# Regrouping tokens at the producers of layer 0's output projection, with norm passes in halves and the next row loaded a step ahead

## The chip, the cores and the metric

The kernel runs on one core of a Trainium2 chip. The metric is the device time of one execution in microseconds (us); lower is better. Engines are named as in the profile: PE is TensorE's matmuls and PEld its weight loads, DVE is VectorE, ACT is ScalarE, POOL is GpSimd, SP is SyncE, which issues all DMAs here.

## The reference, cut to what matters

One inference step of a two-layer recurrent trunk over a prompt of 2048 tokens, model width 1024, and eight single sample tokens, all in float32.

```python
def trunk(x, c, ...):
    for i in range(DEPTH):                       # DEPTH = 2
        shift, scale, gate = split(silu(c) @ mod_w[i] + mod_b[i])
        h = rms_norm(x, norm_w[i]) * (1.0 + scale) + shift
        y = ab_mixer(h, ...) if i % 2 == 0 else s5_mixer(h, ...)
        x = x + gate * y
    return rms_norm(x, final_norm_w), states
```

Layer 0 (`ab_mixer`) projects h to 6160 columns, runs eight RG-LRU heads and eight gated DeltaNet heads along the tokens, gates both with SiLU, and multiplies the 2048 columns of their outputs, y, with an output matrix. Layer 1 (`s5_mixer`) projects h to u and z, runs a diagonal state space model along the tokens, a GLU and an output projection. A final norm follows.

## The kernel before, in words

Activations lie with channels on the 128 partitions and tokens along the free axis, so that a model row of 1024 channels is eight tiles ("rows" k = 0 to 7) of 128 x 1024 tokens. The prompt is worked in two halves of 1024 tokens (`hf`), with the eight sample tokens riding along as columns 1024 to 1031 of one half. The order is: layer 0 for both halves, then layer 1 for both halves.

A float32 matrix product is made of three products of split operands (high and low part of weights and of data). `in_unit` (L863) is one output unit: it multiplies eight rows with eight weight blocks, three products each, for the column blocks in `blocks` (two of 512 columns, or 384, 384 and 264 where the sample columns ride along), accumulates in PSUM (tag "mm", four accumulators) and calls `evac` for each block, which evicts the accumulator. While it issues matmuls it pumps background generators, which trace the recurrences' work in between.

Layer 1's state space model wants the tokens of a half regrouped: instead of their natural order (n t), n = 0 to 127, t = 0 to 7, it wants (t n). Before the change, layer 0 works in natural order, and the regrouping happens in `make_h` (L426) for layer 1: it reads the row x at a step of eight elements (`perm`, L423) and writes h in regrouped order.

`make_h` prepares a stage's input. For each row k it gets x from `xsrc(k)` (which issues a load of 512 KB into a tile "xk"), scales it in place on VectorE (L430), writes the high part hh on ScalarE (L435) and the low part hl on VectorE (L436). It is a generator that yields after each row. `prep0` (L785) calls it for layer 0's second half, `prep1` (L1258) for both halves of layer 1.

Layer 0's outputs go through DRAM. The DeltaNet head's tail (L1158 to L1168) transposes the output back, multiplies it with its gate and stores it to `yd` in two pieces of 512 tokens; `lru` ends (L1205, L1206) with a product of 1024 tokens on POOL and a store to `yd`. `load_y` reads `yd` back and splits it into high and low parts.

`out_phase` (L1222) is the output projection of layer 0, with a first pass over the RG-LRU heads (`grp` 0) and a second over the DeltaNet heads (`grp` 1). Each pass has eight units m. In the first pass `acc[m]` is loaded from the input x; the eviction (L1231) adds gate times the product to it. In the second pass acc[m] is then stored to `x1d`, squared and summed, and after each unit one step (two after the first units) of the next stage's `make_h` is taken. The order of a stage is thus: unit m, store of x1 row m, sum of squares, then step k of `make_h`, whose x load is issued there and used at once. Layer 1's output phase (from L1892) has the same form: x1 row m+1 loaded for the residual, unit m, eviction (L1903, which reads x1 at the step of eight and writes x2 regrouped), sum of squares, store, then a step of `make_h` for the second half.

The program is traced into a tile framework that fixes at build time, from its own estimate of times and a priority that follows the order of tracing, in which order each engine gets its instructions, and gives out the slots of the pools: 35 slots of 1032 x 4 bytes ("a", `TA`), 20 of half the size ("b", `TB`). On the chip every engine's queue, SP's among them, is then worked in that order. `Ahead` (L117) wraps an engine so that its instructions get priority over 2000 others (`VH` is VectorE so wrapped).

Of the kernel before, what the change touches and what calls it, by code (L numbers as in the profile page):

```python
# [70 lines left out]
def hybrid_step(ctx: ExitStack, tc: tile.TileContext, I, O, dump=None):  # L71
# [42 lines left out]
    def dma(out, in_):  # L114
        SP.dma_start(out, in_)  # L115
# [30 lines left out]
    def f(x):  # L146
        return x.bitcast(FT)
# [33 lines left out]
    def wait(n):  # L181
        for _ in range(n):
            yield
# [236 lines left out]
        rsqrt(r, e, (128, 8), "rs8")  # L420
        return r

    def perm(ap):  # L423
        return ap.rearrange("p (n t) -> p t n", t=8)

    def make_h(i, xsrc, rows, hh, hl, permute, w):  # L426

        for k in range(8):
            x = xsrc(k)
            V.scalar_tensor_tensor(x, x, wsc[i][:, k, 0:1], rows, op0=OP.mult, op1=OP.mult)  # L430
            hh[k], hl[k] = TA("hh", FR, (128, w)), TA("hl", FR, (128, w))
            h_, l_ = hh[k][:, 0:HT], hl[k][:, 0:HT]
            if permute:
                x, h_, l_ = perm(x), *(t.rearrange("p (t n) -> p t n", t=8) for t in (h_, l_))
            A.activation(h_, x, AF.Identity, bias=mod[i][:, k, 0:1])  # L435
            V.scalar_tensor_tensor(l_, x, mod[i][:, k, 0:1], f(h_), op0=OP.add, op1=OP.subtract)  # L436
            yield

    def sample_norm(xs, name):
# [345 lines left out]
    def prep0(hf, hh, hl):  # L785
        rows = rows_from_cols(rstd_cols(ss0[hf], "rstd0"), 8)
        yield
        yield from make_h(0, xload(hf), rows, hh, hl, False, HT)

    def load_ba():  # L790
        wba = TB("wba", FT, (128, 8, 32))
# [243 lines left out]
    def gdn_main(hf, h, g):  # L1035
# [120 lines left out]
        rsqrt(ro, m, S8, "rs8")  # L1156
        V.tensor_tensor(o, o, bc(ro[:, :, None], C3), op=OP.mult)
        yield from wait(10)  # L1158
        for b in range(NB):
            ps = PS("pre", Q3)  # L1160
            for c in range(4):
                PE.transpose(ps[:, c, :], o[:, b * 4 + c, :], ident)
            sl = slice(b * 512, (b + 1) * 512)
            y = TB("yb")
            V.scalar_tensor_tensor(y, ps.rearrange("p a b -> p (a b)"), gnw[:, 0:1], zb[:, sl],
                                   op0=OP.mult, op1=OP.mult)
            dma(yd[hf, 8 + h][:, sl], y)
            yield from wait(2)  # L1168


    def lru_split(xc, n):
# [4 lines left out]
    def lru(hf, h, xc, sz, blocks, parts, dc):  # L1176
        (ghi, glo), = W.next()
        n = W1 if hf == 0 else HT
        xh, xl = parts.pop()
        gx, ga, tt = (TA(t_, FT, (128, n)) for t_ in ("gx", "ga", "tt"))  # L1180
        for b0, b1 in blocks:
            pg = [PS("mm", (128, b1 - b0)) for _ in range(2)]
            for j in range(2):
                c = slice(j * 128, j * 128 + 128)
                mm3(pg[j], ghi[:, c], glo[:, c], xh[:, b0:b1], xl[:, b0:b1], True, True)
            A.activation(ga[:, b0:b1], pg[1], AF.Sigmoid, bias=gab[:, h:h + 1])
            A.activation(gx[:, b0:b1], pg[0], AF.Sigmoid, bias=gxb[:, h:h + 1])
        A.activation(tt, ga, AF.Tanh, scale=sp4[:, h:h + 1])
        A.activation(ga, ga, AF.Exp, scale=spm8[:, h:h + 1])
        if dc is not None:  # L1190
            A.activation(dc, dc, AF.Exp)
        A.activation(tt, tt, AF.Sqrt)
        G.tensor_tensor(gx, gx, xc, op=OP.mult)
        V.scalar_tensor_tensor(tt, ga, 1.0, tt, op0=OP.add, op1=OP.mult)
        if hf == 0:
            V.memset(tt[:, 0:1], 1.0)
        G.tensor_tensor(gx, gx, tt, op=OP.mult)
        V.tensor_tensor_scan(tt[:, 0:HT], ga[:, 0:HT], gx[:, 0:HT], lru_h[:, h:h + 1],
                             op0=OP.mult, op1=OP.add)
        V.tensor_copy(lru_h[:, h:h + 1], tt[:, HT - 1:HT])  # L1200
        if hf == 0:
            V.tensor_tensor(slru[:, h, :], slru[:, h, :], ga[:, HT:W1], op=OP.mult)
            V.tensor_tensor(slru[:, h, :], slru[:, h, :], gx[:, HT:W1], op=OP.add)
            V.tensor_tensor(ys[:, h, :], slru[:, h, :], sz[:, HT:W1], op=OP.mult)
        G.tensor_tensor(sz[:, 0:HT], sz[:, 0:HT], tt[:, 0:HT], op=OP.mult)  # L1205
        dma(yd[hf, h], sz[:, 0:HT])  # L1206


    def load_y(hf, grp, yh, yl):
# [12 lines left out]
    def out_phase(hf, grp, blocks, yh, yl, acc, ahead):  # L1222
        sq = Squares()
        for m in range(8):
            if grp == 0:
                acc[m] = TA("acc")
                dma(acc[m], I["xt"][m][:, hf * HT:(hf + 1) * HT])

            def evac(b0, b1, p):
                e = min(b1, HT)  # L1230
                V.scalar_tensor_tensor(acc[m][:, b0:e], p[:, 0:e - b0], mod[0][:, 16 + m, 0:1],  # L1231
                                       acc[m][:, b0:e], op0=OP.mult, op1=OP.add)
                if b1 > HT:
                    t = TT("so", (128, 8))
                    V.tensor_tensor(t, p[:, e - b0:b1 - b0], mod[0][:, 16 + m, 1:9], op=OP.mult)
                    V.tensor_tensor(x1s[:, m, :], x1s[:, m, :], t, op=OP.add)

            in_unit(yh, yl, blocks, evac)
            if grp == 1:
                x1 = acc.pop(m)  # L1240
                dma(x1d[hf, m], x1)
                sq.add(x1)
            if m >= ahead[1]:
                for _ in range(2 if m < ahead[2] else 1):
                    next(ahead[0], None)
        if grp == 1:
            bg.add(finish_later(sq, ss1[hf]), "fin")
        for _ in ahead[0]:
            pass
# [8 lines left out]
    def prep1(hf, hh, hl):  # L1258
        rows = rows_from_cols(rstd_cols(ss1[hf], "rstd1"), 8)
        yield  # L1260
        yield from make_h(1, x1load(hf), rows, hh, hl, True, W1 if hf == 0 else HT)


    def sample0():
# [569 lines left out]
    for hf in range(2):  # L1834
# [64 lines left out]
        def evac_o(m):  # L1899
            def evac(b0, b1, p):  # L1900
                e = min(b1, HT)
                t0, t1 = b0 // 128, e // 128
                V.scalar_tensor_tensor(x2[m][:, b0:e].rearrange("p (t n) -> p t n", n=128),  # L1903
                                       p[:, 0:e - b0].rearrange("p (t n) -> p t n", n=128),
                                       mod[1][:, 16 + m, 0:1], perm(x1[m])[:, t0:t1, :],
                                       op0=OP.mult, op1=OP.add)
                if b1 > HT:
                    V.tensor_copy(Os[:, m, :], p[:, e - b0:b1 - b0])
            return evac
# [59 lines left out]
def layouts(x_prompt, x_sample, c_prompt, c_sample, state_conv_a, state_lru, state_conv_b,  # L1969
# [6 lines left out]
    def cols(v, n):  # L1976
# [5 lines left out]
        "xt": x.T.reshape(8, 128, SEQ),  # L1982
        "xst": x_sample[:, 0].T.reshape(8, 128, 8).transpose(1, 0, 2),
        "ct": np.concatenate([c_prompt, c_sample]).T.reshape(8, 128, 9).transpose(1, 0, 2),
        "modw": mod_w.reshape(2, 4, 2, 128, 6, 512).transpose(0, 4, 1, 3, 2, 5).reshape(2, 6, 4, 128, 1024),
        "modb": mod_b.reshape(2, 24, 128).transpose(2, 0, 1),
        "normw": norm_w.reshape(2, 8, 128).transpose(2, 0, 1),
# [82 lines left out]
```

## Time and profile before

| | us |
|---|---|
| median of 3 runs | 3206.87 |
| the three runs | 3198.5, 3206.87, 3208.52 |
| the profiled execution | 3189.97 |
| span of the profile, first to last instruction | 3188.1 |

The profile is of one execution. TensorE is busy 2953.1 us of the span, VectorE 2089.1, ScalarE 1122.4, POOL 696.7. The mean clock granted to TensorE is 0.966 of full speed. The stages that matter here, in us from the span's start: heads of layer 0, first half, about 75 to 930; its output projection 939 to 1158; heads of the second half to about 2000; its output projection 2011 to 2225; layer 1, first half, to 2727, with its output phase from 2623; layer 1, second half, to the end. Each engine is busy for the time stated, and idle times are given with what ended them; a unit's length is read from the start of its first matmul to the start of the next unit's.

### The profile page before, as it was taken

What the parts mean: (1) busy time and instruction counts of PE and PEld (TensorE: products, weight loads), DVE (VectorE), ACT (ScalarE), POOL (GpSimd) and SP (SyncE); (2) the same over time, 40 slices, a digit from 0 to 9 for tenths busy, and PEclk for the clock granted to TensorE, in tenths of its full rate; (3) what the DMA queues carried; (4) which work ended last, traced back from release to release, by engine and by line L of the source; (5) the groups of instructions that cost most, each with busy time, mean ns of one, the idle gap of its engine ahead of it and who ended that gap; (6) DMA issues with size and microseconds to landing.
All of it is one profiled execution on the core that took longest, in us unless ns stands there. A gap on an engine that the chain in (4) does not pass through costs nothing.

```text
span 3188.1 us, 53992 instructions
## 1 busy us (share of the span) xinstructions
PE 2953.1 (93%) x19958; PEld 2581.2 (81%) x19958; DVE 2089.1 (66%) x5420; ACT 1122.4 (35%) x1999; POOL 696.7 (22%) x672
## 2 busy tenths in 40 slices
PE   5999999999999999999999999998978899988998
PEld 3888888898888777777777778898878899777786
DVE  7896887677885767965766687345555534665525
ACT  3544445444443324433434444223111233201222
POOL 3233433224332322111111121101112222001100
PEclk8999999999989999999999999999989999999999
DMA  6344445344447853444444333565576547597442
GB/s 229 121 133 154 135 140 161 129 135 155 162 134 261 278 188 124 137 132 143 128 131 133 121 115 102 192 207 170 185 218 217 186 151 262 181 311 240 151 138 86
DMA packets 406440, 532.09 MB, mean 167 GB/s; under 512 B 143776, under 2 KB 210848, under 8 KB 406176
## 3 DMA queue, kind: packets, MB, share of 16 engines
q1 hardware_dynamic: 406176, 528.63, 50.8%
q8 instruction: 158, 2.59, 0.3%
q14 instruction: 106, 0.87, 0.1%
HBM read 328.11 MB, written 200.36 MB: 166 GB/s over the span
## 4 chain that ended last, share of the span: by engine, by line
PE 55%; DVE 27%; DMA 7%; issue 4%; ACT 3%; POOL 2%; SPq 2%; DVEq 0%; POOLq 0%; ACTq 0%
PE ps_mm L874 41%; DVE s5t L127 4%; DVE c_v L854 2%; DMA xk<-x1d 2%; SPq L115 2%; DVE xc L854 1%; DVE fsP L1002 1%; DVE c_q L854 1%; PE ps_pre L1783 1%; DVE fsT L1004 1%; ACT hh L435 1%; POOL wlo L234 1%; PE ps_pre L1725 1%; PE ps_ch L1137 1%; PE ps_pre L1782 1%
## 5 line engine op out<-in xcount | busy, mean ns | idle before, releaser
L874 PE MATMUL ps_mm<-hh,wlo 128*128 128x512 f32 (+2 forms) x2536 | 792.1, 373 | 0.0
L874 PE MATMUL ps_mm<-hh,whi 128*128 128x512 f32 (+2 forms) x2536 | 761.7, 361 | 4.4 <-DVE sz L1868 2.0
L874 PE MATMUL ps_mm<-hl,whi 128*128 128x512 f32 (+2 forms) x2536 | 748.7, 355 | 0.8 <-DVE hl L436 0.8
L874 PEld LDWEIGHTS ps_mm<-hl,whi 128*128 128x128 f32 x2536 | 479.6, 192 | 45.3 <-DVE hl L436 1.2
L874 PEld LDWEIGHTS ps_mm<-hh,whi 128*128 128x128 f32 x2536 | 472.6, 192 | 54.0 <-DVE sz L1868 2.5
L874 PEld LDWEIGHTS ps_mm<-hh,wlo 128*128 128x128 f32 x2536 | 449.9, 192 | 35.7 <-issue 7.4
L234 POOL TENSOR_TENSOR wlo<-wraw,whi 128x512 fp32r<-128x512 f32 (+1 forms) x200 | 280.9, 1411 | 639.1 <-ACT whi L233 408.4
L874 PE MATMUL ps_mm<-yh,whi 128*128 128x512 f32 (+2 forms) x640 | 187.2, 360 | 16.0 <-DVE acc L1231 8.0
L874 PE MATMUL ps_mm<-yl,whi 128*128 128x512 f32 (+2 forms) x640 | 189.1, 357 | 2.9 <-DVE yl L234 2.9
L874 PE MATMUL ps_mm<-yh,wlo 128*128 128x512 f32 (+2 forms) x640 | 190.8, 361 | 0.0
L233 ACT ACTIVATE whi<-wraw 128x512 fp32r<-128x512 f32 (+1 forms) x200 | 121.7, 617 | 104.4 <-DMA wraw<-in_w 47.6
L1134 ACT ACTIVATE qs<-ps_ch,geg 128x128 f32<-128x128 f32 x128 | 47.1, 368 | 287.6 <-DVE rr L1131 284.2
L874 PEld LDWEIGHTS ps_mm<-yh,whi 128*128 128x128 f32 x640 | 119.7, 192 | 29.5 <-ACT yh L233 9.3
L854 DVE SCALAR_TENSOR_TENSOR c_k<-raw,cbw,c_k 128x256 f32<-128x256 f32 x192 | 92.0, 517 | 63.3 <-ACT c_k L891 62.4
L874 PEld LDWEIGHTS ps_mm<-yl,whi 128*128 128x128 f32 x640 | 120.9, 192 | 15.3 <-DVE yl L234 3.9
L874 PEld LDWEIGHTS ps_mm<-yh,wlo 128*128 128x128 f32 x640 | 119.0, 192 | 9.7
L874 PE MATMUL ps_mm<-y2h,whi 128*128 128x384 f32 (+3 forms) x344 | 102.6, 345 | 7.4 <-DVE x L1903 7.4
L890 ACT ACTIVATE raw<-ps_mm 128x384 f32<-128x384 f32 (+1 forms) x160 | 81.6, 513 | 72.7 <-PE ps_mm L874 69.2
L874 PE MATMUL ps_mm<-y2h,wlo 128*128 128x384 f32 (+3 forms) x344 | 101.8, 345 | 0.0
L874 PE MATMUL ps_mm<-y2l,whi 128*128 128x384 f32 (+3 forms) x344 | 101.4, 344 | 0.0
L854 DVE SCALAR_TENSOR_TENSOR xc<-raw,caw,xc 128x256 f32<-128x256 f32 x192 | 95.6, 519 | 4.2 <-ACT xc L891 3.6
L854 DVE SCALAR_TENSOR_TENSOR c_v<-raw,cbw,c_v 128x256 f32<-128x256 f32 x192 | 95.4, 531 | 4.0 <-ACT c_v L891 3.8
(669 smaller groups left out, 5772.3 us busy)
## 6 DMA issues: line engine op xcount, KB each, us to landing
wraw<-in_w SPq DMA_DIRECT2D x128, 256.0 KB, 3.7
whw<-whi SPq DMA_DIRECT2D x128, 256.0 KB, 2.6
wlw<-wlo SPq DMA_DIRECT2D x128, 256.0 KB, 2.3
whi<-whw SPq DMA_DIRECT2D x128, 256.0 KB, 4.5
wlo<-wlw SPq DMA_DIRECT2D x128, 256.0 KB, 4.5
modw<-in_modw SPq DMA_DIRECT2D x48, 512.0 KB, 5.6
yk<-yd SPq DMA_DIRECT2D x32, 512.0 KB, 6.0
xk<-x1d SPq DMA_DIRECT2D x32, 512.0 KB, 5.4
```

What stands on the lines that cost most here:

```text
L115: SP.dma_start(out, in_)
L127: return getattr(self.eng, op)(*args, **kw)
L233: a = A.activation(hi, src, AF.Identity)
L234: return a, (lo_eng or V).tensor_tensor(lo, src, f(hi), op=OP.subtract)
L435: A.activation(h_, x, AF.Identity, bias=mod[i][:, k, 0:1])
L854: V.scalar_tensor_tensor(d, raw[:, a * n + j:a * n + j + n], wt[:, tile_i, j:j + 1], d, op0=OP.mult, op1=OP.add)
L874: PE.matmul(p, w[:, c], x[:, b0:b1], start=(k == 0 and x is hh[k] and w is wh), stop=(k == 7 and w is wl))
L890: A.activation(raw[:, 3 + b0:3 + e], p[:, 0:e - b0], AF.Copy)
L1002: V.tensor_tensor(pr_[:, 0:i, 0:i], Ti[:, 0:i, 0:i].rearrange("p j c -> p c j"), bc(F[:, 0:i, i].unsqueeze(1), s), op=OP.mult)
L1004: V.tensor_reduce(Ti[:, i, 0:i], pr_[:, 0:i, 0:i], axis=AX.X, op=OP.add, negate=True)
L1134: A.activation(qs, p1[:, 1, :], AF.Copy, scale=g["eg"][:, c:c + 1])
L1137: PE.matmul(p2_, U[:, c, :], rr, start=True, stop=True)
```

## The change

`make_h` no longer permutes. It issues the load of row k+1 before it works on row k, and works each row in two halves of 512 tokens. The tokens are regrouped earlier: the DeltaNet tail and the RG-LRU end write their outputs in (t n) order, that is with a step of 128 elements (512 bytes) between neighbours in time, and `acc` is loaded from `xp`, a copy of x that the host lays out in (t n) order. The DeltaNet tail collects both halves in one tile of the big pool and stores it with one DMA of 512 KB. The RG-LRU product goes to `gx` instead of `sz`. Both evictions (L1231, L1903) are issued through `VH`, and the one of layer 1 loses its permuted operand.

```diff
-    def perm(ap):
-        return ap.rearrange("p (n t) -> p t n", t=8)
-
-    def make_h(i, xsrc, rows, hh, hl, permute, w):
-
+    def by_t(ap):
+        return ap.rearrange("p (n t) -> p n t", t=8)
+
+    def make_h(i, xsrc, rows, hh, hl, w):
+
+        nxt = xsrc(0)
         for k in range(8):
-            x = xsrc(k)
-            V.scalar_tensor_tensor(x, x, wsc[i][:, k, 0:1], rows, op0=OP.mult, op1=OP.mult)
+            x = nxt
+            if k < 7:
+                nxt = xsrc(k + 1)
             hh[k], hl[k] = TA("hh", FR, (128, w)), TA("hl", FR, (128, w))
-            h_, l_ = hh[k][:, 0:HT], hl[k][:, 0:HT]
-            if permute:
-                x, h_, l_ = perm(x), *(t.rearrange("p (t n) -> p t n", t=8) for t in (h_, l_))
-            A.activation(h_, x, AF.Identity, bias=mod[i][:, k, 0:1])
-            V.scalar_tensor_tensor(l_, x, mod[i][:, k, 0:1], f(h_), op0=OP.add, op1=OP.subtract)
+            for c in (slice(0, HT // 2), slice(HT // 2, HT)):
+                x_, h_, l_ = x[:, c], hh[k][:, c], hl[k][:, c]
+                V.scalar_tensor_tensor(x_, x_, wsc[i][:, k, 0:1], rows[:, c], op0=OP.mult, op1=OP.mult)
+                A.activation(h_, x_, AF.Identity, bias=mod[i][:, k, 0:1])
+                V.scalar_tensor_tensor(l_, x_, mod[i][:, k, 0:1], f(h_), op0=OP.add, op1=OP.subtract)
             yield
...
+        y = TA("yb")
         for b in range(NB):
...
-            y = TB("yb")
-            V.scalar_tensor_tensor(y, ps.rearrange("p a b -> p (a b)"), gnw[:, 0:1], zb[:, sl],
+            V.scalar_tensor_tensor(y.rearrange("p (t n) -> p n t", t=8)[:, b * 64:(b + 1) * 64],
+                                   by_t(ps.rearrange("p a b -> p (a b)")), gnw[:, 0:1], by_t(zb[:, sl]),
                                    op0=OP.mult, op1=OP.mult)
-            dma(yd[hf, 8 + h][:, sl], y)
             yield from wait(2)
+        dma(yd[hf, 8 + h], y)
...
-        G.tensor_tensor(sz[:, 0:HT], sz[:, 0:HT], tt[:, 0:HT], op=OP.mult)
-        dma(yd[hf, h], sz[:, 0:HT])
+        G.tensor_tensor(gx[:, 0:HT].rearrange("p (t n) -> p n t", t=8), by_t(sz[:, 0:HT]), by_t(tt[:, 0:HT]),
+                        op=OP.mult)
+        dma(yd[hf, h], gx[:, 0:HT])
...
-                dma(acc[m], I["xt"][m][:, hf * HT:(hf + 1) * HT])
+                dma(acc[m], I["xp"][m][:, hf * HT:(hf + 1) * HT])
...
-                V.scalar_tensor_tensor(acc[m][:, b0:e], p[:, 0:e - b0], mod[0][:, 16 + m, 0:1],
+                VH.scalar_tensor_tensor(acc[m][:, b0:e], p[:, 0:e - b0], mod[0][:, 16 + m, 0:1],
...
-                t0, t1 = b0 // 128, e // 128
-                V.scalar_tensor_tensor(x2[m][:, b0:e].rearrange("p (t n) -> p t n", n=128),
-                                       p[:, 0:e - b0].rearrange("p (t n) -> p t n", n=128),
-                                       mod[1][:, 16 + m, 0:1], perm(x1[m])[:, t0:t1, :],
-                                       op0=OP.mult, op1=OP.add)
+                VH.scalar_tensor_tensor(x2[m][:, b0:e], p[:, 0:e - b0], mod[1][:, 16 + m, 0:1],
+                                        x1[m][:, b0:e], op0=OP.mult, op1=OP.add)
...
+        "xp": x.T.reshape(8, 128, 2, 128, 8).transpose(0, 1, 2, 4, 3).reshape(8, 128, 2048),
```

## Rows read from the trace of the kernel before

**Rows 1.** The page's first part: busy us (share of the span) and instructions of each engine.
```profile
PE 2953.1 (93%) x19958; PEld 2581.2 (81%) x19958; DVE 2089.1 (66%) x5420; ACT 1122.4 (35%) x1999; POOL 696.7 (22%) x672
```

**Rows 2.** The page's chain that ended last: share of the span by engine.
```profile
PE 55%; DVE 27%; DMA 7%; issue 4%; ACT 3%; POOL 2%; SPq 2%; DVEq 0%; POOLq 0%; ACTq 0%
```

**Rows 3.** Windows of units, layer 0's last output pass: length, busy (instructions) by engine, PEclk, DMA.
```profile
2145.40:2156.75 11.35, 11.35 (x74) 11.35 (x73) 6.47 (x8) 2.69 (x3) 0.00 (x0) 1.00 0.71 233
...
2168.10:2180.92 12.82, 11.59 (x75) 11.32 (x73) 7.60 (x10) 4.02 (x4) 1.28 (x1) 1.00 0.49 159
...
2192.59:2205.20 12.61, 11.59 (x75) 11.32 (x73) 6.23 (x9) 4.36 (x4) 4.08 (x2) 1.00 0.49 166
2205.20:2225.19 19.99, 14.20 (x75) 13.93 (x74) 9.73 (x13) 6.59 (x5) 3.85 (x2) 0.83 0.55 170
```

**Rows 4.** Windows of units, output phase of layer 1's first half.
```profile
2634.14:2645.48 11.34, 11.34 (x74) 11.34 (x73) 2.68 (x4) 3.71 (x6) 3.85 (x3) 1.00 0.95 311
...
2656.82:2671.96 15.14, 13.17 (x74) 12.90 (x73) 8.15 (x8) 5.15 (x5) 5.59 (x3) 0.89 0.82 282
2671.96:2684.55 12.59, 11.60 (x74) 11.34 (x73) 5.50 (x8) 4.05 (x3) 2.66 (x2) 1.00 0.72 252
2684.55:2700.19 15.64, 13.16 (x75) 12.90 (x73) 9.75 (x9) 3.38 (x2) 0.00 (x0) 0.89 0.52 171
...
2711.79:2727.02 15.23, 13.32 (x75) 12.98 (x73) 9.30 (x9) 3.38 (x2) 0.00 (x0) 0.89 0.43 139
```

**Rows 5.** Waits of PE, 2130 to 2226, then 2625 to 2745: total us, times, longest.
```profile
PE ps_mm L874 <- DVE acc L1231: 8.0, 3, 5.8
...
PE ps_mm L874 <- DVE x L1903: 7.4, 4, 2.5
```

**Rows 6.** Timeline of DVE in the longest unit: start, length, instruction, idle before it.
```profile
2205.15 1.28 DVE L430 SCALAR_TENSOR_TENSOR xk<-xk,wsc,rows 128x1024 f32<-128x1024 f32 x1 [2.92 <-DMA xk<-x1d]
2208.69 2.05 DVE L436 SCALAR_TENSOR_TENSOR hl<-xk,mod,hh 128x1024 fp32r<-128x1024 f32 x1 [2.26 <-ACT hh L435]
2210.67 1.52 DVE L1231 SCALAR_TENSOR_TENSOR acc<-ps_mm,mod,acc 128x384 f32<-128x384 f32 x3
```

**Rows 7.** Timeline of SP's queue before it.
```profile
2199.55 0.38 SPq L115 DMA_DIRECT2D x1d<-acc  x1
2199.99 0.43 SPq L115 DMA_DIRECT2D xk<-x1d  x1
```

**Rows 8.** Groups by form, 1080 to 1175, ACT: busy us, mean ns of one | idle before.
```profile
L435 ACT ACTIVATE hh<-xk,mod 128x1024 fp32r<-128x1024 f32 x8 | 9.2, 1152 | 36.8 <-DVE xk L430 28.5 <-DMA whi<-whw 8.2
```

**Rows 9.** Groups by form, 2630 to 2746.
```profile
L435 ACT ACTIVATE hh<-xk,mod 128x1024 fp32r<-128x1024 f32 x8 | 18.6, 2327 | 40.7 <-DVE xk L430 40.7
...
L436 DVE SCALAR_TENSOR_TENSOR hl<-xk,mod,hh 128x1024 fp32r<-128x1024 f32 x8 | 17.7, 2218 | 19.0 <-ACT hh L435 19.0
...
L1903 DVE SCALAR_TENSOR_TENSOR x<-ps_mm,mod,xk 128x384 f32<-128x384 f32 x16 | 14.6, 958 | 13.8 <-PE ps_mm L874 7.4 <-DMA wraw<-in_wo 6.4
```

**Rows 10.** Groups by form, whole span, DVE.
```profile
L1165 DVE SCALAR_TENSOR_TENSOR yb<-ps_pre,gnw,zbl 128x512 f32<-128x512 f32 x32 | 23.9, 746 | 13.9 <-PE ps_pre L1162 13.7
...
L1231 DVE SCALAR_TENSOR_TENSOR acc<-ps_mm,mod,acc 128x384 f32<-128x384 f32 x32 | 18.5, 611 | 14.9 <-PE ps_mm L874 9.1 <-DMA wlo<-wlwo 5.5
```

**Rows 11.** Timeline of DVE at the end of the program.
```profile
3173.52 1.42 DVE L1953 TENSOR_TENSOR x<-x,rows 128x256 f32<-128x256 f32 x4
3174.87 0.66 DVE L1903 SCALAR_TENSOR_TENSOR x<-ps_mm,mod,xk 128x256 f32<-128x256 f32 x1
```

**Rows 12.** The instructions of line 1205: shortest, median, longest ns; first and last start.
```profile
L1205 POOL TENSOR_TENSOR sz<-sz,tt x16: 2334/2373/2877, 165.2 to 2002.4; 128x1024 f32<-128x1024 f32 x16
```

**Rows 13.** Timelines of SP's queue and of PE where the second half's heads end.
```profile
2004.76 0.32 SPq L115 DMA_DIRECT2D yd<-sz  x1
...
2011.54 1.23 PE L874 MATMUL ps_mm<-yh,whi 128*128 128x384 f32 x3 [3.97 <-ACT yh L233]
```

**Rows 14.** The instructions on the tile yk: shortest, median, longest ns.
```profile
L234 DVE TENSOR_TENSOR yl<-yk,yh x32: 1217/1232/2315, 942.0 to 2129.0; 128x1024 fp32r<-128x1024 f32 x16, 128x1032 fp32r<-128x1032 f32 x16
```

More of the change, by code (lines that the diff above doesn't have):

```diff
@@ L787, in prep0 @@
         yield
-        yield from make_h(0, xload(hf), rows, hh, hl, False, HT)
+        yield from make_h(0, xload(hf), rows, hh, hl, HT)
     def load_ba():
@@ L1260, in prep1 @@
         yield
-        yield from make_h(1, x1load(hf), rows, hh, hl, True, W1 if hf == 0 else HT)
+        yield from make_h(1, x1load(hf), rows, hh, hl, W1 if hf == 0 else HT)
     def sample0():
```

## The prediction, made before the changed kernel was run

> **What bounds the kernel now.** The page's first part comes first: TensorE is busy 93% of the span [rows 1], so a gain must come from stretches in which it stands still. The chain of waits gives 55% to TensorE and 27% to VectorE [rows 2]; TensorE's queue is thus not the only one that sets the end. To find where the change can act I cut the two stages that it rewrites into output units (72 matmuls each: 8 k by 3 products by 3 column blocks). A unit that nobody disturbs, the first row of each group, takes 11.35 us in the last output stage of layer 0 and 11.34 us in the first one of layer 1 [rows 3, 4]. [...] The list of TensorE's waits says for whom: VectorE's eviction of the accumulators, 8.0 us in three waits and 7.4 us in four [rows 5]. [...]
>
> Why is an eviction late? In the worst case VectorE first waits 2.92 us for an x row, scales it, waits 2.26 us for ScalarE's hh, spends 2.05 us on hl, and only then evicts [rows 6]. Its queue is in order, so the eviction is queued behind all that. The x row is late because its load was issued at 2199.99 us, right behind the store of the unit before, some 5 us ahead of its use [rows 7]. hh and hl read the row at a step of eight elements: 2327 ns on ScalarE against 1152 ns for the same instruction without the step [rows 8, 9], and 2218 ns on VectorE [rows 9].
>
> **The change part by part.**
>
> *Rows loaded one step ahead, in halves, unpermuted* (one answer). The load of row k+1 is now issued when step k begins, a unit earlier (11.35 us) than its use, against some 5 us of flight [rows 6, 7]: the 2.92 us wait goes. Each step issues four VectorE instructions of 512 elements in place of two of 1024, and two on ScalarE in place of one. A VectorE instruction of this kind and size takes 746 ns [rows 10], so a step costs 4 x 0.75 = 3.0 us, against 1.28 + 2.22 = 3.5 us now [rows 6, 9]; ScalarE's half takes about 1152 / 2 = 0.6 us (an estimate from rows 8). The longest thing that an eviction can find ahead of it in the queue falls from 2.9 + 1.3 + 2.3 + 2.1 = 8.5 us to about 0.75 + 0.6 + 0.75 = 2.1 us. What may it be? The first two blocks of a unit are complete when the third, 264 of 1032 columns, starts; that is about 264 / 1032 x 11.35 = 2.9 us before the next unit wants the first accumulator back (four accumulators for three blocks a unit). 2.1 is under 2.9, so these stalls should end. SP's queue gets as many loads as before, each earlier by one step; the next weights' loads stand behind them as they do now.
>
> *Eviction without permutation and with priority.* A 384-column eviction that reads x1 with the step takes 958 ns [rows 9], the one in the other layer without it 611 ns [rows 10]: (958 - 611) / 384 = 0.90 ns an element for the strided operand. The 43 evictions of layer 1 become shorter by 0.2 to 0.5 us; that lies beside TensorE and counts for nothing by itself except at the end. Priority puts an eviction ahead of other VectorE work that is ready when the order is drawn up. The cover for both is TensorE's running unit.
>
> Gain in the first stage: 12.82 - 11.35 = 1.47, 12.61 - 11.35 = 1.26, 19.99 - 11.35 = 8.64, together 11.4 us [rows 3]. In the second: 3.80 + 1.25 + 4.30 + 3.89 = 13.2 us [rows 4]. At the very end the last eviction stands behind four row scalings of 1.42 us together [rows 11], of which priority saves between nothing and all, so half, and is itself strided (256 x 0.90 ns): 0.7 + 0.2 = 0.9 us. Together **25.5 us**. The output stage of the first half of the tokens works on unpermuted rows today, and none of its waits is counted.
>
> *Where the regrouping goes.* The producers write it now. VectorE's gated output (32 instructions of 512 elements, 746 ns each [rows 10]) gets a destination with a step of 512 bytes, and so do 16 products of 1024 elements on POOL, 2373 ns each [rows 12]. No row shows a strided write of this kind, so: at least nothing more, for the write may hide behind the two reads; a gain has no reason, since nothing is left out. At most twice the time, as ScalarE's read with the step does (2327 / 1152 [rows 8, 9]). For VectorE I take the strided read of the same kind, 0.90 ns an element, 0.46 us each, 14.7 us over 32; for POOL the same per element, 0.92 us each. What is hidden? While heads run TensorE has matmuls of the next head, and VectorE has 27% of the chain [rows 2]: I put 0.27 x 14.7 = 4.0 us on the path. POOL's products are waited for only where a half of the heads ends: the store of the last one stands ahead of the next stage's loads in SP's queue, and TensorE then waits 3.97 us for the first row [rows 13]. Two such ends give 2 x 0.92 = 1.8 us. One store of 512 KB replaces two of 256 KB (one issue less for each head); it starts after the second half, and the rows are read back stages later, so I cost it at nothing, as I do the acc rows from another input tensor of the same size and shape.
>
> [...] The trace shows 0.90 ns more an element for a strided read [rows 9, 10]. [...]
>
> **Sum.** 25.5 - 4.0 - 1.8 = 19.7 us less. Against the profiled execution's own time of 3189.97 us (span 3188.1) that is 3170.3. That execution was 16.9 us quicker than the median of the three runs, 3206.87; I set the difference against the median: **3187 us**.
>
> **The rivals.**
> 1. *No room for the row ahead.* The pool of big tiles has 35 slots. In the first stage 16 hold y, up to 16 hh and hl, and the rows, the squares and the accumulators left over want the rest, so in the last steps the row ahead may get its slot no sooner than now. Then the last unit of each stage keeps its excess (8.64 and 3.89), 12.5 us: 3207 - 7.3 = 3200. For it: loads already go out right behind a store [rows 7]. Against it: in the second stage the late units lie in the middle too [rows 4].
> 2. *The priority does not do what it says:* where the planner thinks an eviction is not ready yet, it still places it behind the halves, and half of the 24.6 us stays: 3207 - 7.5 = 3199. Against it: what is placed ahead has become short.
> 3. *The writers pay in full; slower.* Strided writes double both producers: 32 x 0.75 + 16 x 2.37 = 24 + 38 = 62 us [rows 10, 12] in the loops over heads. From 35 us of it on the path the gain is gone (25.5 + 9.6), with three quarters on it (46 us) the time is 3207 + 21 = 3228. For it: a VectorE instruction with two operands in SBUF can stretch from 1232 to 2315 ns [rows 14], and a longer POOL product would give more of that. Against it: only 27% of the chain is VectorE's and 2% POOL's [rows 2]. [...]
>
> **How the numbers follow.** About 0.3% (9.6 us) is what a measurement of this kernel can tell from no change. Forecast 0.62, nearly all beyond that bound; rival 1 0.14 and rival 2 0.12, mostly within it; rival 3 0.12, nearly all slower. This gives faster 0.63, same 0.25, slower 0.12. The range: with no cost for the writes the median is 3181, and a set of runs can lie lower by the 16.9 us between profile and median, which gives 3165; at the top all of the gain fails and the writes cost 5.8 us, 3213. Left out above is most of rival 3.
>
> **What would show it.** Right: the units of both stages at 11.3 to 11.5 us with a granted clock of 1.00; TensorE's waits for L1231 and L1903 under 2 us in total; hl and hh in halves near 0.75 and 0.6 us; x rows landed before VectorE asks. Wrong: yb well over 1.2 us or the POOL product over 3.3 us; VectorE still waiting for x rows in the last steps; a longer stretch from 75 to 930 us or from 1180 to 2000 us than now; or another order of the heads' work moving the time by more than these terms.

## The result, and the profile after

| | before | changed |
|---|---|---|
| median in the first comparison, us | 3207.7 (4 runs, 3198.5 to 3208.5) | 3162.65 (4 runs, 3162.5 to 3165.1) |
| the profiled execution, us | 3189.97 | 3162.53 |
| output projection of layer 0, second half, both passes (stage A), us | 213.49 | 203.22 |
| output phase of layer 1's first half (stage B), us | 104.06 | 91.10 |

The medians lie 45 us apart. The estimated ratio of the two times is 0.9877, 95% interval 0.9853 to 0.9902, which is 31 to 47 us. The forecast was 3187 us, with 3165 as its low end; the direction held, the size did not. Between the two profiled executions the difference is 27.4 us, and 10.3 + 13.0 = 23.2 us of it lie in the two stages that the prediction named. The stages are measured from the first matmul of one to the first of the next.

First the page of the changed kernel, its busy times and its chain, beside [rows 1, 2]:

```profile
PE 2946.8 (93%) x19958; PEld 2577.6 (82%) x19958; DVE 2077.0 (66%) x5468; ACT 1109.6 (35%) x2023; POOL 689.1 (22%) x672
...
PE 57%; DVE 26%; DMA 7%; issue 4%; ACT 2%; POOL 2%; SPq 2%; DVEq 0%; POOLq 0%; ACTq 0%
```

TensorE has the same instructions and is busy 6.3 us less. The long units of [rows 3, 4] alone were busy 9.2 us beyond the quiet ones, nearly all of it in those with a granted clock under 1.00. Then the windows of the units of stage A, which answer to [rows 3] (length; busy time and instructions of PE, PEld, DVE, ACT and POOL; granted clock; DMA share; GB/s):

```profile
2165.55:2176.86 11.31, 11.31 (x74) 11.31 (x73) 5.92 (x10) 3.44 (x5) 1.28 (x1) 1.00 0.56 181
...
2188.17:2199.49 11.32, 11.32 (x75) 11.32 (x73) 5.44 (x10) 3.56 (x5) 2.60 (x3) 1.00 0.65 232
2199.49:2210.96 11.47, 11.47 (x75) 11.47 (x74) 6.61 (x10) 3.03 (x4) 1.92 (x2) 1.00 0.59 194
```

and those of stage B, which answer to [rows 4]:

```profile
2655.83:2667.18 11.35, 11.35 (x75) 11.35 (x73) 5.79 (x8) 3.44 (x5) 3.46 (x3) 1.00 0.89 295
2667.18:2678.85 11.67, 11.61 (x74) 11.34 (x73) 6.36 (x11) 2.29 (x3) 0.00 (x0) 1.00 0.83 315
2678.85:2690.20 11.35, 11.35 (x75) 11.35 (x73) 5.57 (x9) 2.29 (x3) 0.00 (x0) 1.00 0.67 231
```

In the last unit of stage A before, the granted clock was 0.50 from 2210 to 2216 us and 1.00 from 2217 on, and pairs of 384-column matmuls took 0.84 us in the first stretch and 0.51 in the second. That unit went from 19.99 to 11.47 us, at a granted clock of 1.00 in place of 0.83; the units of 15.14 and 15.64 us in stage B have become 11.35 to 11.67. The waits of TensorE for an eviction, 8.0 and 7.4 us in [rows 5], are gone from the list of stage A and sum to 0.06 us in stage B.

So far this is the forecast. The list of VectorE's waits is not. Before (2108 to 2230, then 2606 to 2730; total us, times, longest):

```profile
DVE xk L430 <- DMA xk<-x1d: 21.0, 6, 5.7
DVE hl L436 <- ACT hh L435: 13.7, 8, 2.5
...
DVE xk L430 <- DMA xk<-x1d: 18.6, 6, 3.6
DVE hl L436 <- ACT hh L435: 14.5, 6, 2.4
```

The changed kernel, same stretches (make_h's lines are now L436 to L438):

```profile
DVE xk L436 <- DMA xk<-x1d: 15.2, 5, 4.2
...
DVE hl L438 <- ACT hh L437: 0.2, 1, 0.2
...
DVE xk L436 <- DMA xk<-x1d: 20.3, 7, 4.3
```

**VectorE waits for the x row nearly as before**: 15.2 against 21.0 us in stage A and 20.3 against 18.6 us in stage B, although each row's load is issued one step ahead. (Both lists of stage B go by the same clock; the changed kernel's stage ends at 2701.5, and without the step behind it the wait is 19.1 us.) What is gone is the wait for hh. The timeline of VectorE in stage B shows what this does; first before (start, length, instruction, idle before it):

```profile
2680.71 1.29 DVE L430 SCALAR_TENSOR_TENSOR xk<-xk,wsc,rows 128x1024 f32<-128x1024 f32 x1 [3.61 <-DMA xk<-x1d]
2684.43 2.08 DVE L436 SCALAR_TENSOR_TENSOR hl<-xk,mod,hh 128x1024 fp32r<-128x1024 f32 x1 [2.43 <-ACT hh L435]
2686.44 2.33 DVE L1903 SCALAR_TENSOR_TENSOR x<-ps_mm,mod,xk 128x384 f32<-128x384 f32 x3
```

and TensorE's timeline beside it:

```profile
2687.37 0.44 PE L874 MATMUL ps_mm<-y2h,whi 128*128 128x384 f32 x1 [2.48 <-DVE x L1903]
```

then the changed kernel (evictions issued through the priority wrapper have its line, L127):

```profile
2658.79 2.49 DVE L438 SCALAR_TENSOR_TENSOR hl<-xk,mod,hh 128x512 fp32r<-128x512 f32 x2
2665.59 1.41 DVE L436 SCALAR_TENSOR_TENSOR xk<-xk,wsc,rows 128x512 f32<-128x512 f32 x2 [4.30 <-DMA xk<-x1d]
2666.92 1.53 DVE L127 SCALAR_TENSOR_TENSOR x<-ps_mm,mod,xk 128x384 f32<-128x384 f32 x3
```

with SP's queue ahead of it:

```profile
2658.11 0.38 SPq L115 DMA_DIRECT2D x2d<-x  x1
2658.55 2.42 SPq L115 DMA_DIRECT2D xk<-x1d  x2
```

Before, 2686.44 - 2680.71 = 5.7 us lie between the landing of the row and the eviction, and TensorE stands 2.48 us. In the changed kernel it is 2666.92 - 2665.59 = 1.3 us, and TensorE stands 0.06 us. The row awaited at 2665.59 is that of the load issued 7 us earlier, at 2658.55; the load before it, issued at 2647.66, had long been there (the longest flight of a row in this stage is 7.5 us). So VectorE's order has moved ahead along with the load: it does hl of the row before while the row is in flight, and scales the new row as soon as it lands. I call the stretch from the row's landing to the eviction **the tail**. It was the tail that the change cut, not the wait.

What the instructions cost now, by form (busy us, mean ns of one | idle before), VectorE over the whole span:

```profile
L438 DVE SCALAR_TENSOR_TENSOR hl<-xk,mod,hh 128x512 fp32r<-128x512 f32 x48 | 38.0, 820 | 4.8 <-DMA x1d<-acc 3.7 <-ACT hh L437 0.2
L1167 DVE SCALAR_TENSOR_TENSOR yb<-ps_pre,gnw,zbl 128x512 f32<-128x512 f32 x32 | 36.7, 1148 | 13.0 <-PE ps_pre L1165 11.4 <-issue 1.5
L436 DVE SCALAR_TENSOR_TENSOR xk<-xk,wsc,rows 128x512 f32<-128x512 f32 x48 | 35.4, 769 | 44.2 <-DMA xk<-x1d 35.5 <-DMA xk<-in_xt 8.7
```

and POOL's product, shortest, median and longest ns, as in [rows 12]:

```profile
L1208 POOL TENSOR_TENSOR gx<-sz,tt x16: 2362/2390/2910, 165.1 to 2002.5; 128x1024 f32<-128x1024 f32 x16
```

The strided write costs VectorE 1148 - 746 = 0.40 us for 512 elements [rows 10]. POOL's product has a median of 2390 ns against 2373 [rows 12]: there the same step costs 17 ns for 1024.

### The profile page after: what moved, and what is told of

The parts are those of the page before. It is cut to its first block, busy times and chain, and to the rows that moved or that the text cites. A ratio compares the mean times of both kernels' runs of the same rounds, so it can differ in the third digit from the quotient of the medians.

```text
span 3160.6 us, 54048 instructions
## 1 busy us (share of the span) xinstructions
PE 2946.8 (93%) x19958; PEld 2577.6 (82%) x19958; DVE 2077.0 (66%) x5468; ACT 1109.6 (35%) x2023; POOL 689.1 (22%) x672
## 4 chain that ended last, share of the span: by engine, by line
PE 57%; DVE 26%; DMA 7%; issue 4%; ACT 2%; POOL 2%; SPq 2%; DVEq 0%; POOLq 0%; ACTq 0%
PE ps_mm L876 44%; DVE s5t L127 4%; DVE c_v L856 2%; SPq L115 2%; DVE xc L856 1%; DVE fsP L1004 1%; DMA yk<-yd 1%; DVE c_q L856 1%; DVE fsT L1006 1%; PE ps_pre L1787 1%; POOL wlo L234 1%; DVE D L910 1%; PE ps_ch L1139 1%; PE ps_ch L1145 1%; PE ps_pre L1786 1%
```

## The experiments

The kernels ran in three groups, and the kernel before beside each: its median was 3195.0 us in the first (e1 to e4), 3192.6 in the second (e5 to e8) and 3200.6 in the third (e9 to e12). The first two groups ran on one chip, the third on another. The theory was that evictions are late because of what stands ahead of them in VectorE's queue, and that the profiled execution of before was only a quick one of its kind. The questions: which of the four parts does it, what do the strided writes cost, and why 45 us when the stages give 23.

**e1: the kernel before once more**, no edit.

> The kernel before, unchanged, once more, to see what an execution near 3207 us spends more than the profiled one of 3190. Theory A (the late x rows cost a varying time): the extra 10 to 18 us lie in the two output stages, whose disturbed units then take longer than the 11.4 and 13.2 us of excess found, and nowhere else. Rival B (something that runs through the whole program, such as the start or the loads of layer 1): the extra time lies outside these two stages. If this execution is again near 3190, it settles nothing.

3196.3 us (10 runs, 3184.8 to 3212.7), ratio 1.0003 (0.9983 to 1.0023). Its profiled execution took 3196.48 us, 6.5 more than the first, and stages A and B took 214.03 and 104.53 us, 1.0 us more together. Of these 6.5 us, 5.5 thus lie outside the two stages, which speaks against theory A; it is one trace, and of an execution that is not as slow as 3207 us.

**e2: only the row loaded ahead**, on the kernel before:

```diff
+        nxt = xsrc(0)
         for k in range(8):
-            x = xsrc(k)
+            x = nxt
+            if k < 7:
+                nxt = xsrc(k + 1)
```

> The kernel before with the next x row loaded one step ahead, and nothing else of the change. Theory A (the x row's load is what keeps VectorE's queue standing): most of both stages' excess goes, 8 to 20 us less than the kernel before. Rival C (the length of the strided hl and hh is what keeps evictions late): at most 5 us less, and units of 12 to 15 us stay.

3174.1 us, ratio 0.9938 (0.9919 to 0.9957); stages 202.45 and 96.55 us. VectorE's timeline in a unit of stage B:

```profile
2672.41 2.29 DVE L439 SCALAR_TENSOR_TENSOR hl<-xk,mod,hh 128x1024 fp32r<-128x1024 f32 x1 [1.04 <-ACT hh L438]
2675.30 1.58 DVE L433 SCALAR_TENSOR_TENSOR xk<-xk,wsc,rows 128x1024 f32<-128x1024 f32 x1 [0.60 <-DMA xk<-x1d]
2676.80 1.88 DVE L1906 SCALAR_TENSOR_TENSOR x<-ps_mm,mod,xk 128x384 f32<-128x384 f32 x2
```

The tail is 1.5 us with rows still permuted. hl, still long, now fills the flight of the next row, so the wait for rows falls to 5.5 us in stage B. One stall is left, 4.4 us, in the step where the loading ahead begins: there two rows are scaled one after the other before hl, and the tail is 5.55 us. In time (21 us less) theory A came true.

**e3: only the priority**, on the kernel before:

```diff
-                V.scalar_tensor_tensor(acc[m][:, b0:e], p[:, 0:e - b0], mod[0][:, 16 + m, 0:1],
+                VH.scalar_tensor_tensor(acc[m][:, b0:e], p[:, 0:e - b0], mod[0][:, 16 + m, 0:1],
...
-                V.scalar_tensor_tensor(x2[m][:, b0:e].rearrange("p (t n) -> p t n", n=128),
+                VH.scalar_tensor_tensor(x2[m][:, b0:e].rearrange("p (t n) -> p t n", n=128),
```

> The kernel before with both evictions given priority, and nothing else. Theory A: an eviction is still behind an x row that is late on the chip but not in the planner's estimate, so at most 8 us less. Rival D (the order in VectorE's queue is the cause, and priority alone mends it): 15 us less or more, with units near 11.4 us.

3194.4 us, ratio 0.9991 (0.9977 to 1.0005); stages 212.16 and 102.58 us. TensorE's waits in the two stages, beside [rows 5]:

```profile
PE ps_mm L874 <- DVE acc L127: 6.8, 3, 5.7
...
PE ps_mm L874 <- DVE x L127: 10.4, 5, 2.8
```

The time did not change: the evictions still stand behind the step of make_h, and rival D fell.

**e4: only the regrouping at the producers** (the changed kernel without the row ahead, the halves and the priority):

```diff
-        nxt = xsrc(0)
         for k in range(8):
-            x = nxt
-            if k < 7:
-                nxt = xsrc(k + 1)
+            x = xsrc(k)
...
-            for c in (slice(0, HT // 2), slice(HT // 2, HT)):
+            for c in (slice(0, HT),):
...
-                VH.scalar_tensor_tensor(acc[m][:, b0:e], p[:, 0:e - b0], mod[0][:, 16 + m, 0:1],
+                V.scalar_tensor_tensor(acc[m][:, b0:e], p[:, 0:e - b0], mod[0][:, 16 + m, 0:1],
...
-                VH.scalar_tensor_tensor(x2[m][:, b0:e], p[:, 0:e - b0], mod[1][:, 16 + m, 0:1],
+                V.scalar_tensor_tensor(x2[m][:, b0:e], p[:, 0:e - b0], mod[1][:, 16 + m, 0:1],
```

> The changed kernel with x rows loaded at their step, worked whole, and evictions without priority: of the change only the regrouping at the producers is left. Theory A: VectorE still waits for x rows, so the longest unit of layer 0's last output stage stays over 14 us; 5 to 15 us less than the kernel before. Rival C (length of the strided operations): 20 us less or more, and units near 11.4 us.

3173.9 us, ratio 0.9929 (0.9905 to 0.9953); stages 205.93 and 92.93 us. Its VectorE waits 23.5 us for rows in stage B, more than before's 18.6, and yet only 1.6 and 1.3 us of waits for an eviction are left in the two stages. Theory A of this run missed (the longest unit of stage A is 13.1 us, not over 14, and the gain is 21 us); rival C has the time. The timeline of its worst step in stage B:

```profile
2668.39 1.29 DVE L433 SCALAR_TENSOR_TENSOR xk<-xk,wsc,rows 128x1024 f32<-128x1024 f32 x1 [5.05 <-DMA xk<-x1d]
2670.90 1.28 DVE L435 SCALAR_TENSOR_TENSOR hl<-xk,mod,hh 128x1024 fp32r<-128x1024 f32 x1 [1.23 <-ACT hh L434]
2672.10 1.53 DVE L1903 SCALAR_TENSOR_TENSOR x<-ps_mm,mod,xk 128x384 f32<-128x384 f32 x3
```

and TensorE's there, in the first matmuls of the next unit, which began at 2671.38:

```profile
2668.45 0.29 PE L873 MATMUL ps_mm<-y2h,whi 128*128 128x264 f32 x1
...
2672.77 0.45 PE L873 MATMUL ps_mm<-y2h,whi 128*128 128x384 f32 x1 [1.06 <-DVE x L1903]
```

This is the slack at work. The first two blocks are complete when the third starts, at 2668.45; the next unit starts at 2671.38, 2.9 us later, and takes its second block's accumulator at once. The row landed at 2668.39; the tail of 3.7 us and the first eviction of 0.6 end at 2672.7, and TensorE stood 1.06 us. With before's tail of 5.7 and its eviction of 0.96 [rows 9] it would have stood 3.4 (an estimate from these figures).

**e5: the changed kernel once more**, no edit.

> The changed kernel, unchanged, beside the kernel before on the chip of this call. The two stages' gain is 24 us between the profiles, the whole 27. Theory E (the kernel before's time differs from execution to execution and from chip to chip by 10 us or more, and that is the rest of the 45 us): 25 to 35 us less than the kernel before here. Rival F (the change gives 45 us everywhere): 40 us less or more.

3163.5 us (3158.8 to 3169.7) beside 3192.6 for before: ratio 0.9909 (0.9885 to 0.9932), 29 us. The changed kernel came out as the first time; before came out 15 us lower, as theory E had it. But this trace of the changed kernel is not free of stalls. Stages A and B took 205.23 and 94.96 us, and one unit of stage B was long:

```profile
2664.72:2680.25 15.53, 13.06 (x74) 12.79 (x73) 8.04 (x13) 2.29 (x3) 0.00 (x0) 0.89 0.73 279
```

VectorE and TensorE there:

```profile
2665.53 1.41 DVE L436 SCALAR_TENSOR_TENSOR xk<-xk,wsc,rows 128x512 f32<-128x512 f32 x2 [6.71 <-DMA xk<-x1d]
2666.86 1.53 DVE L127 SCALAR_TENSOR_TENSOR x<-ps_mm,mod,xk 128x384 f32<-128x384 f32 x3
...
2667.53 0.69 PE L876 MATMUL ps_mm<-y2h,whi 128*128 128x384 f32 x1 [2.47 <-DVE x L127]
```

The tail is 1.3 us, as in the first trace. But the row landed 3.75 us after the first two blocks were complete (2661.78), where the first trace has 1.34 us (2665.59 and 2664.24): its load was issued 4.7 us after the start of the unit then running, in place of 2.7. So a late row can still cost, whatever the tail.

**e6: the changed kernel without the row ahead** (the first part of e4's diff).

> The changed kernel with each x row loaded at its own step again. Theory G (unpermuted short operations alone bring the eviction under its slack of about 2.9 us, so either remedy is enough): within 6 us of the changed kernel, VectorE still waiting some 4 us for each x row, units at 11.3 to 12 us. Rival A (the late row is the cause): 10 us or more slower than the changed kernel.

3165.9 us, ratio 0.9909 (0.988 to 0.9939), so theory G holds; stages 201.56 and 91.03 us, though VectorE waits 27.0 and 23.3 us for rows in them. One step of stage B:

```profile
2663.71 1.41 DVE L433 SCALAR_TENSOR_TENSOR xk<-xk,wsc,rows 128x512 f32<-128x512 f32 x2 [5.23 <-DMA xk<-x1d]
2665.25 1.42 DVE L435 SCALAR_TENSOR_TENSOR hl<-xk,mod,hh 128x512 fp32r<-128x512 f32 x2
2666.59 1.53 DVE L127 SCALAR_TENSOR_TENSOR x<-ps_mm,mod,xk 128x384 f32<-128x384 f32 x3
```

In halves the wait for hh is gone: hl starts 0.13 us after the scaling (2665.25 - 2663.71 - 1.41), where half an hh takes 0.71 us in the changed kernel, so ScalarE works on one half while VectorE scales the other. That leaves a tail of 2.9 us, and a stall of 0.15 us in this step. The row ahead is not needed once the tail is this short.

**e7: the changed kernel without the priority** (the third and fourth part of e4's diff).

> The changed kernel with both evictions at the usual priority. Theory G: within 4 us of the changed kernel, units at 11.3 to 11.5 us. Rival D (priority matters once the operations are short): 6 us or more slower, with units of 12 us and more in the two stages.

3164.0 us, ratio 0.9921 (0.9894 to 0.9948); stages 205.16 and 91.30 us. No difference in time, as e3 had it from the other side: one step of stage B has a tail of 4.6 us where the changed kernel has 2.9, and costs a stall of 0.25 us.

**e8 and e9: the changed kernel with whole rows** (the second part of e4's diff), in two groups.

> The changed kernel with rows worked whole (two VectorE instructions of 1.28 us and one of 1.15 us on ScalarE a step) in place of halves. Theory G: within 4 us of the changed kernel, since 1.28 + 1.2 + 1.28 us ahead of an eviction are just above its slack. Rival H (the halves are what makes it fit): 6 us or more slower, with units of 12 us and more.

> The changed kernel with each row worked whole instead of in two halves, run a second time, now beside the changed kernel itself. The first time it came out at 3154.3 us where the changed kernel had 3163.5 in the same call. Theory H (the halves cost more than they give: six instructions a row in place of three): 6 to 12 us under the changed kernel of this call again. Theory J (the 9 us were the scatter between executions, 3158.8 to 3169.7 against 3152.6 to 3160.1, which nearly meet): within 4 us of it.

3154.3 us (3152.6 to 3160.1) in the second group, 9 us under the changed kernel; 3169.2 us (3154.2 to 3179.1) in the third, 6 us over it. The ratios to before are 0.9881 (0.9864 to 0.9898) and 0.9909 (0.9888 to 0.9929). Neither theory of e9 met its bounds; the 9 us were scatter. Whole rows or halves make no difference that was repeated, and there was no version here that surely beats the changed kernel.

**e10: whole rows and no priority**, so the regrouping and the row ahead alone (the last three parts of e4's diff).

> Whole rows and no priority on the two evictions: what is left is the regrouping at the producers and the row loaded a step ahead, the smallest version that has both remedies. If priority does nothing here either (as in the two runs that added it alone and took it alone away), it is within 4 us of the whole rows with priority. If the longer instructions of whole rows make priority worth something, 5 us or more slower, with units over 12 us in the two output stages.

3165.1 us (3161.5 to 3171.5), ratio 0.9893 (0.9878 to 0.9908); stages 203.95 and 91.20 us. The same as with everything.

**e11: DeltaNet outputs written contiguously**, in the changed kernel:

```diff
-            V.scalar_tensor_tensor(y.rearrange("p (t n) -> p n t", t=8)[:, b * 64:(b + 1) * 64],
-                                   by_t(ps.rearrange("p a b -> p (a b)")), gnw[:, 0:1], by_t(zb[:, sl]),
+            V.scalar_tensor_tensor(y[:, sl],
+                                   ps.rearrange("p a b -> p (a b)"), gnw[:, 0:1], zb[:, sl],
```

> The changed kernel, but the DeltaNet heads write their gated outputs in natural order (leaves out the regrouping of these 1024 columns of y; the RG-LRU heads and the rest stay). The 32 writes should fall from about 1148 to about 746 ns, 12.9 us of VectorE. Prediction's own term: 0.27 of it on the path, 3.5 us faster than the changed kernel. Theory W0 (hidden beside the next head's matmuls): within 2 us. Rival 3 (in full on the path): 12 to 13 us faster, all of it in the two stretches of the heads.

3162.5 us, ratio 0.9887 (0.9869 to 0.9904), beside 3163.6 and 0.9893 for e12. The writes did become short again (shortest, median, longest ns):

```profile
L1167 DVE SCALAR_TENSOR_TENSOR yb<-ps_pre,gnw,zbl x32: 729/746/752, 265.8 to 2092.5; 128x512 f32<-128x512 f32 x32
```

32 x 0.40 = 12.9 us of VectorE are saved, and about 1 us of time, within the uncertainty: the strided writes of the heads are hidden beside TensorE's work on the next head.

**e12: the changed kernel a third time**, no edit.

> The changed kernel, as the measure for the three others of this call. Theory E (before's base moves from call to call, the changed kernel's less): 3158 to 3170 us, and 25 to 35 us under the kernel before. Theory F (the 45 us of the first comparison are real): 40 us or more under it.

3163.6 us (3158.4 to 3183.2) beside 3200.6 for before: ratio 0.9893 (0.9872 to 0.9914), 37 us, between what the two theories asked for. Stages A and B took 203.80 and 92.38 us.

Now the stalls side by side. The wait for rows is VectorE's in stage B. Landing, tail and stall are those of the worst step of stage B; the landing is counted from the completion of the unit's first two blocks (the start of its third block), and so is the end of the first eviction, which gives an accumulator back. All in us:

| kernel | wait for rows | landing | tail | first eviction ends | stall | A | B |
|---|---|---|---|---|---|---|---|
| before | 18.6 | -0.91 | 5.72 | 5.70 | 2.48 | 213.49 | 104.06 |
| e2, row ahead alone | 5.5 | 1.15 | 5.55 | 7.60 | 4.38 | 202.45 | 96.55 |
| e4, regrouped alone | 23.5 | -0.06 | 3.71 | 4.27 | 1.06 | 205.93 | 92.93 |
| e6, no row ahead | 23.3 | -0.14 | 2.88 | 3.36 | 0.15 | 201.56 | 91.03 |
| changed | 19.1 | 1.34 | 1.33 | 3.28 | 0.06 | 203.22 | 91.10 |
| e5, changed again | 18.3 | 3.75 | 1.33 | 5.69 | 2.47 | 205.23 | 94.96 |

The stall is not set by the sum of the waits, and not by the tail alone. It is what landing, tail and first eviction together exceed 3.2 us by: that is the slack, 2.9 us to the start of the next unit and 0.3 more until its second block's turn. This holds in stage B of all 14 traces: 28 of 112 units end in a stall, each of them the excess over 3.20 to 3.27 us, and no unit without one exceeds 3.23.

Either remedy alone takes most steps to within about a microsecond of the slack or under it; the second one finds little left. In the two stages the row ahead alone gives 18.6 us, the regrouping alone 18.7, and both together 17.4 to 23.2 in the three traces of the changed kernel, against the first trace of before. In time it is 21 us each alone (3195.0 - 3174.1 and 3195.0 - 3173.9), and 29 to 45 us together, of which the part beyond the stages is not explained.

## Why the prediction was right and where it failed

- **What bounds the kernel, and where the change acts**: right. In the first trace of the changed kernel both stages came down to quiet units, at a granted clock of 1.00; e5's has one unit of 15.53 us left, e12's three of 11.9 to 12.3.
- **Gain in the stages**: forecast 11.4 and 13.2 us, measured 10.3 and 13.0. At the end 0.9 was forecast; from the last output phase's first matmul to the end it was 110.4 us before and 110.3 after, so that term came to nothing. Together 23.3 of 25.5 us; with e5's and e12's traces in place of the first it would be 17 and 21 us in the stages.
- **"The 2.92 us wait goes"**: this step failed. Loads issued a step earlier were also used a step earlier, since VectorE's order is drawn up at build time and put the scaling of the new row ahead of the evictions. The wait for rows stayed at 15.2 and 19.1 us, one of the prediction's own signs of being wrong. The longest thing ahead of an eviction is thus not 2.1 us, as the prediction had it, but a wait of 4.3 and a scaling of 1.4. The sum itself was the wrong measure: it set all that stands ahead of an eviction against the slack, whereas only what comes after the completion of the block counts, that is the landing, the tail and the eviction. The slack was forecast as 2.9 us and measured as 3.2. That the late rows did no harm in the first trace (3.28 us) is in part luck: in e5's the same step came to 5.69 us and cost a stall of 2.47.
- **Halves**: hl at 0.75 us (747 ns in the middle, 820 in the mean) as forecast; hh took 0.71 us where half of 1152 ns was estimated.
- **Cost of the strided writes**: for VectorE 0.40 us each in place of 0.46, a good bound from the strided read. On the path 4.0 us were forecast and e11 shows about 1, within the uncertainty; nor did the two stretches of heads get longer together, for the second half's output projection began at 2007.6 us in place of 2011.5. VectorE's share of the chain, 27%, is no price for work that lies beside the next head's matmuls. For POOL 0.92 us each was forecast and 0.02 measured (2390 against 2373 ns). The same step of 512 bytes thus shows in VectorE's writes, 402 ns on 746, and hardly in POOL's, 17 ns on 2373.
- **The base**: the second step that failed, and the larger term. The difference was set against 3206.87, the median of three runs. The 42 executions of before that ran beside the changed kernels and their variants have a median of 3197.0 us (3186.9 to 3208.5), so the three were 10 us high, and the profiled execution, which looked 16.9 us quick, was 7 us quick. The changed kernel's 14 executions have a median of 3163.0 (3158.4 to 3183.2): 34 us less. From 3197.0, less the 25.5 us at no cost for the writes, the forecast would have been 3171.5, still 8 us too high. Whether the chip or the executions made the 10 us is not shown: 3195.0 and 3192.6 come from one chip, 3200.6 from another.
- **Rivals**: the first (no room for the row ahead) foresaw the symptom, rows as late as now, with another cause, and priced it at 12.5 us, where it cost nothing in the first trace and about 4 us in e5's. The second is right about priority (e3 and e7), but the gain did not hang on it. The third fell: 62 us of longer producers turned out to be 12.9 us, hidden. Of the 32 instructions of [rows 14], the four long ones (1.63 to 2.32 us) began while a TENSOR_TENSOR of POOL was running, and the 22 with no POOL instruction beside them took 1.22 to 1.24; the 32 gated outputs took 730 to 753 ns in the trace of before, 12 of them with a TENSOR_TENSOR of POOL beside them.

**What stays open.** Of the 34 us, 17 to 24 lie in the two stages, by two traces of before against three of the changed kernel. The other 10 to 17 are not settled. Outside the stages the span is 2870.5 and 2876.0 us in two profiled executions of before, and 2866.3, 2861.1 and 2867.3 us in three of the changed kernel, which points the same way; but the variants that regroup have 2858 (e9) to 2880 us (e4) there, so single executions spread over more than the difference, and no term of the change was shown to act there.

## What to carry to other kernels

Where an eviction is queued behind a step that waits for a load, measure three things: when the load lands, the tail from there to the eviction, and the slack that the accumulators leave. TensorE stood here by what landing, tail and first eviction exceeded the slack of 3.2 us by. Cutting the tail (5.72 to 1.33 us in the worst step) took the stalls of stage B from 7.4 to 0.06 us while the wait stayed (18.6 and 19.1 us), but a row that landed 3.75 us after the first two blocks still cost 2.47 us at the same tail (e5). A second remedy for the same tail added little here (18.6 and 18.7 us each alone in the two stages, 17.4 to 23.2 together), so its gain must not be added. And before a difference of one per cent is set against a time, look at the spread of the executions: three of them stood 10 us off here.

## What the runs showed that I had not expected

- A write with a step of 512 bytes cost VectorE 54% more (746 to 1148 ns for 512 elements) and POOL under 1% (2373 to 2390 ns for 1024).
- In the changed kernel, loading earlier did not make a row arrive earlier relative to its use: 19.1 us of waits in stage B against 18.6, because the instructions that use it moved with it. In e2, where the long hl fills the flight, the wait fell to 5.5 us.
- Executions of one program differ by over 20 us (3184.8 to 3212.7 in ten of e1, the kernel before), while stages A and B differ by about 0.5 us each between the two traces of that kernel; between those of the changed kernel stage B differs by up to 3.9 us, for one late row.
